# Two of three pairs of FFN input tiles as seven block products in place of eight, with the sums on VectorE and two accumulators to a PSUM bank

## The chip, the cores and the metric

The kernel runs on one core of one Trainium2 chip. The metric is the device time of one execution in microseconds (us). Three runs of the kernel before took 1320.02, 1320.15 and 1322.49 us; the median is 1320.15 us. The engines are TensorE (PE in the rows; PEld is its weight load), VectorE (DVE), ScalarE (ACT), GpSimd (POOL) and SyncE (SP), whose queue starts most transfers.

## The reference

One decoder layer on 512 tokens of width 1024 in float32: an FFN, a token mixer, a second FFN and an embedding stage, each with norms and a residual. The change is in the two FFNs:

```python
def rmsnorm(x, g):
    y = x * rsqrt(mean(x * x, axis=-1, keepdims=True) + EPS)
    return y * g

def swiglu(u, w_in, w_out):            # u 512x1024, w_in 1024x5632, w_out 2816x1024
    gate, up = split(u @ w_in, 2, axis=-1)
    return (silu(gate) * up) @ w_out

h = h + 0.5 * rmsnorm(swiglu(rmsnorm(h, ffn1_norm_pre), ffn1_w_in, ffn1_w_out), ffn1_norm_post)
h = h + rmsnorm(token_mixer(rmsnorm(h, mix_norm_pre), ...), mix_norm_post)
h = h + 0.5 * rmsnorm(swiglu(rmsnorm(h, ffn2_norm_pre), ffn2_w_in, ffn2_w_out), ffn2_norm_post)
```

## The kernel before, in words

**Three matmuls for one.** Every float32 operand is held as two parts, a rounded high part and the rest: `whi`/`wlo` of a weight chunk, `uhi`/`ulo` of the normed input. `wchunk` (L83) loads a chunk of 128x1024 over SP's queue into one of two `raw` buffers, ScalarE casts the high part (L91) and VectorE subtracts it for the low part (L92). `mm3` (L99) adds high by high, high by low and low by high into PSUM.

**The FFN.** `ffn` (L247) computes 22 pairs of tiles, f = 0 to 21: a gate tile and an up tile, each 128 hidden columns by 512 tokens. A tile takes one weight chunk: eight blocks of 128 input rows, three matmuls each, 24 matmuls of 512 columns into one bank (`pgu`, L282). `ev` (L252) follows: ScalarE applies Silu to the gate tile (L259), VectorE multiplies the up tile in (L262), ScalarE casts and VectorE subtracts the two parts of `hid` (L263, L266). The first tile pairs of an FFN (three in the first FFN, two in the second) go through `start_tiles` (L223) instead, token half by token half, in matmuls of 256 columns (tile `p` in the rows), because the input arrives by token blocks.

**The output projection.** `out_proj` (L168) multiplies `hid` by `wo`, two column halves of 11 chunks each; the first half takes the chunks as they come, with the parts in `vhi`/`vlo`, two buffers. Each chunk feeds 24 matmuls. The residual `h`, 512x1024, lies in SBUF (`h`, tag `hz`) through the FFN, and the two gain rows are loaded while f = 4 runs.

**What sets the order.** The program is written tile by tile, and a scheduler places the instructions of each engine into one list; each engine works through its list in order, and so does SP's queue. A buffer is written again when its last reader is done. PSUM has eight banks: four for tag `mm`, four for tag `ax`.

Of the kernel before, what the change touches and what calls it, by code (L numbers as in the profile page):

```python
# [32 lines left out]
def layer_kernel(ctx, tc, x, pT, wf1, wo1, wfm, wsm, wtm, wbr, wout, wf2, wo2, wgate, wproj,  # L33
# [198 lines left out]
    def sandwich_tail(h, ys, gn, u):  # L232
        def finish(tt, r):
            V.scalar_tensor_tensor(h[:, tt, :], ys[tt], r, h[:, tt, :], op0=ALU.mult, op1=ALU.add)
            make_u(tt, h, gn, u, ys[tt])
        return finish

# [9 lines left out]
    def ffn(fp, free, wf, wo, h, u, gi, gn_i, first):  # L247
        hid = [None] * FT
        marks = []
        g = {}  # L250

        def ev(f, part):  # L252
            def run(n, ps):
                if part == 0:
                    if f == 2 and len(first) == 6:
                        t = g[f] = lp.tile([128, T + 608], F32, name="gx")
                    else:
                        t = g[f] = sp.tile([128, T], F32, name="gt", tag="t512", bufs=2)
                    A.activation(t[:, n], ps[:, n], AF.Silu)  # L259
                else:  # L260
                    t = g[f]
                    V.tensor_tensor(t[:, n], ps[:, n], t[:, n], op=ALU.mult)  # L262
                    m = A.copy(hid[f][:, 0, n], t[:, n])  # L263
                    if f == 4:
                        marks.append(m)
# [9 lines left out]
        start_tiles([(w, 128, ev(i // 2, i % 2)) for i, w in enumerate(first)], u)  # L275
        for f in range(nf, FT):
            hid[f] = hid_tile(f)
            for i in range(2):
                w = wchunk(wf[2 * f + i])
# [12 lines left out]

        def load(ch, j, a):
            if a is None:
                dst = upper(fp)
# [7 lines left out]
        return u2  # L303

    hdram = dp.tile([128, 4, D], F32, name="hdram")
    gd = dp.tile([16, 128, T], F32, name="gd")
# [5 lines left out]
    with pool("s1", "right") as small:  # L312
        env.small = small
        f1_pool = ExitStack()
        fp = f1_pool.enter_context(pool("f1"))
        xt = [small.tile([128, D], F32, name=f"ys{i}") for i in range(2)]
        SY.dma_start(h[:, 0, :], x[0])
        SY.dma_start(cst[:, 0:C_TRI], consts[:, 0:C_TRI])
        SY.dma_start(h[:, 1, :], x[1])
        gn = small.tile([128, D], F32, name="gn")  # L320
        SY.dma_start(gn, gain_row(G_F1))
        weights = start_weights(fp, wf1, 6, 2)
        first = [next(weights)]
# [12 lines left out]
        u = ffn(fp, f1_pool.close, wf1, wo1, h, u, G_F1 + 1, G_MIX, first)  # L336
        for tt in range(4):
            SY.dma_start(hdram[:, tt, :], h[:, tt, :])

# [620 lines left out]
    if True:  # L960
        tl = tail_pool.enter_context(pool("tail"))
        mgh = tl.tile([128, KT, T], F32R, name="mgh")
        mgl = tl.tile([128, KT, T], F32R, name="mgl")
        gpt = small.tile([128, D], F32, name="gp")
        gnt = small.tile([128, D], F32, name="gn")
        ys = [small.tile([128, D], F32, name=f"ys{tt}") for tt in range(4)]
        h = hp.tile([128, 4, D], F32, name="h2", tag="hz")
        for tt in range(4):
            SY.dma_start(h[:, tt, :], hdram[:, tt, :])
        for m2 in range(4):  # L970
            wb = wchunk(wbr[4 + m2], dst=upper(tl))
# [149 lines left out]
```

## Time and profile before

| | us |
|---|---|
| median of three runs | 1320.15 |
| the profiled execution | 1320.2 |
| its span in the trace | 1318.4 |
| TensorE busy | 1287.5 |
| VectorE busy | 639.3 |
| ScalarE busy | 465.7 |

The span runs from the first instruction to the last; 1.8 us of the execution lie around it. The granted TensorE clock was 0.994 of full speed over the span. Matmuls are pipelined: a matmul's own duration holds the time in the pipe, and successive ones overlap. What a stream of them costs is read from the distance between their starts, or between events that stand once in each tile.

### The profile page before, as it was taken

To read this page: it belongs to the slowest core of one execution; us is meant where nothing else is said; L and a number is where in the kernel's file an instruction comes from. 1 tells how busy PE (TensorE), PEld (TensorE's weight loads), DVE (VectorE), ACT (ScalarE), POOL (GpSimd) and SP (SyncE) were. 2 spreads that over 40 slices of the span, in tenths; PEclk is the share of its full clock that TensorE was granted. 3 is DMA by queue.
4 is the path that set the end of the run, shared out by engine and by line. 5 is a ranking of instruction groups with operands and counts; after the bars stand their busy time and mean duration, and the time that the engine had idled before them with its cause. 6 is when DMAs were issued, how large, how long until landed. Compare 5 with 4: busy or idle time off the path is not lost.

```text
span 1318.4 us, 16647 instructions
## 1 busy us (share of the span) xinstructions
PE 1287.5 (98%) x6661; PEld 1074.3 (81%) x6661; DVE 639.3 (48%) x1088; ACT 465.7 (35%) x765; POOL 70.0 (5%) x71
## 2 busy tenths in 40 slices
PE   7999999999989999999999999989999999999997
PEld 6988888888879888877678888779888888888876
DVE  6233333323262699987686454463333333223465
ACT  6222222212253453454655222352222223112353
POOL 0000000000010000021002001220000000000000
PEclk9999999999999999999999999999999999999999
DMA  6243333223342223344206635522433333233431
GB/s 216 67 128 96 96 96 98 94 83 99 122 143 92 88 65 111 97 121 130 79 1 147 212 108 181 159 87 81 130 96 96 96 96 108 68 96 96 128 112 64
DMA packets 57772, 141.26 MB, mean 107 GB/s; under 512 B 17568, under 2 KB 20064, under 8 KB 57696
## 3 DMA queue, kind: packets, MB, share of 16 engines
q1 hardware_dynamic: 56688, 136.54, 33.9%
q10 hardware_dynamic: 1008, 3.67, 0.9%
q8 instruction: 52, 0.85, 0.3%
q14 instruction: 24, 0.20, 0.0%
HBM read 128.62 MB, written 11.57 MB: 106 GB/s over the span
## 4 chain that ended last, share of the span: by engine, by line
PE 86%; DMA 5%; DVE 5%; ACT 2%; issue 1%; POOL 0%; SPq 0%; DVEq 0%; POOLq 0%; ACTq 0%
PE pgu L101 11%; PE pgu L100 11%; PE pgu L102 11%; PE acc L101 5%; PE acc L102 5%; PE acc L100 5%; PE p L101 3%; PE p L100 3%; PE p L102 3%; PE ptm L101 2%; PE ptm L100 2%; PE ptm L102 2%; PE pg L100 2%; PE pg L102 2%; PE pg L101 2%; PE pat L713 2%
## 5 line engine op out<-in xcount | busy, mean ns | idle before, releaser
L91 ACT CAST whi<-raw 128x1024 fp32r<-128x1024 f32 x135 | 142.1, 1052 | 389.7 <-PE pgu L101 154.0
L92 DVE TENSOR_TENSOR wlo<-raw,whi 128x1024 fp32r<-128x1024 f32 x135 | 166.3, 1232 | 195.0 <-ACT whi L91 187.6
L100 PE MATMUL pgu<-uhi,whi 128*128 128x512 f32 x624 | 242.8, 389 | 0.0
L102 PE MATMUL pgu<-uhi,wlo 128*128 128x512 f32 x624 | 242.8, 389 | 0.0
L101 PE MATMUL pgu<-ulo,whi 128*128 128x512 f32 x624 | 242.7, 389 | 0.0
L100 PEld LDWEIGHTS pgu<-uhi,whi 128*128 128x128 f32 x624 | 117.1, 188 | 24.5
L102 PEld LDWEIGHTS pgu<-uhi,wlo 128*128 128x128 f32 x624 | 117.1, 188 | 24.4
L101 PEld LDWEIGHTS pgu<-ulo,whi 128*128 128x128 f32 x624 | 117.1, 188 | 24.0
L92 DVE TENSOR_TENSOR vlo<-raw,vhi 128x1024 fp32r<-128x1024 f32 x45 | 56.1, 1249 | 131.0 <-ACT vhi L91 130.9
L101 PE MATMUL acc<-vlo,hid 128*128 128x512 f32 x288 | 112.1, 389 | 0.0
L102 PE MATMUL acc<-vhi,hid 128*128 128x512 f32 x288 | 111.7, 389 | 0.0
L91 ACT CAST vhi<-raw 128x1024 fp32r<-128x1024 f32 x45 | 47.1, 1048 | 143.7 <-PE acc L102 123.3
L100 PE MATMUL acc<-vhi,hid 128*128 128x512 f32 x288 | 97.4, 389 | 0.0
L262 DVE TENSOR_TENSOR gt<-pgu,gt 128x512 f32<-128x512 f32 x39 | 27.0, 692 | 136.7 <-PE pgu L102 136.7
L78 POOL TENSOR_TENSOR rinv<-ms,mhalf 128x1 f32<-128x1 f32 x32 | 18.9, 594 | 844.0 <-DVE ms L123 844.0
L101 PEld LDWEIGHTS acc<-vlo,hid 128*128 128x128 f32 x288 | 54.1, 188 | 11.3
L100 PEld LDWEIGHTS acc<-vhi,hid 128*128 128x128 f32 x288 | 54.1, 188 | 11.2
L102 PEld LDWEIGHTS acc<-vhi,hid 128*128 128x128 f32 x288 | 54.0, 188 | 11.3
L101 PE MATMUL ptm<-wlo,uhi 128*128 128x512 f32 x128 | 50.3, 393 | 0.0
L100 PE MATMUL ptm<-whi,uhi 128*128 128x512 f32 x128 | 50.0, 395 | 0.0
L102 PE MATMUL ptm<-whi,ulo 128*128 128x512 f32 x128 | 49.8, 391 | 0.0
L100 PE MATMUL pg<-uhi,whi 128*128 128x512 f32 x104 | 41.2, 396 | 0.0
(394 smaller groups left out, 2335.9 us busy)
## 6 DMA issues: line engine op xcount, KB each, us to landing
raw<-wf SPq DMA_DIRECT2D x88, 512.0 KB, 3.6
raw<-wo SPq DMA_DIRECT2D x44, 512.0 KB, 3.6
raw<-wfm SPq DMA_DIRECT2D x28, 512.0 KB, 3.7
raw<-wtm SPq DMA_DIRECT2D x20, 512.0 KB, 3.7
gd<-gst SPq DMA_DIRECT2D x16, 256.0 KB, 2.1
raw<-wbr SPq DMA_DIRECT2D x8, 512.0 KB, 4.4
grl<-gd SPq DMA_DIRECT2D x16, 256.0 KB, 3.2
raw<-wout SPq DMA_DIRECT2D x8, 512.0 KB, 4.2
```

Source lines behind the costliest of these rows:

```text
L78: G.tensor_tensor(out_, in_, e, op=ALU.pow)
L91: A.copy(hi[:, :n], raw[:, :n])
L92: (eng or V).tensor_sub(lo[:, :n], raw[:, :n], hi[:, :n].bitcast(F32))
L100: PE.matmul(ps, l[0], r[0], start=start, stop=False)
L101: PE.matmul(ps, l[0], r[1], start=False, stop=False)
L102: PE.matmul(ps, l[1], r[0], start=False, stop=stop)
L262: V.tensor_tensor(t[:, n], ps[:, n], t[:, n], op=ALU.mult)
L713: PE.matmul(pa[:, :S], qbT[b:b + 64, pr, tt * 128:tt * 128 + 128], kbT[b:b + 64, pr, :S], start=True, stop=True)
```

## The change

Of f = 4 to 21, those with f % 3 = 0 stay as they were (6, 9, ... 21), and the other twelve of each FFN go through the new `Seven.pair`. There the gate chunk is cut into g1 (input rows 0 to 511) and g2 (512 to 1023), the up chunk into w1 and w2, and the input into b11, b21 (tokens 0 to 255) and b12, b22 (tokens 256 to 511). With

- S1 = w1 + w2, S2 = S1 - g1, S3 = g1 - w1, S4 = g2 - S2 (tiles `sa` and `sb`)
- T1 = b12 - b11, T2 = b22 - T1, T3 = T2 - b11, T4 = b21 - T2 (once per FFN, in `Seven.__init__`)

the seven products are g1 b11, g2 b21, S2 T2, S3 T3, S1 T1, w2 T4 and S4 b22, each of four blocks by three matmuls of 256 columns. They land in `pa` to `pd` (in the rows `pfa` to `pfd`), two to a bank but for the first, and VectorE adds them into `ct`. The parts are made by `parts`: ScalarE casts, VectorE subtracts. x1 are the parts of the gate chunk, x2 of `sa`, x3 of `sb`, x4 of w2.

Buffers: the parts take turns over three `whi`/`wlo` sets and one set in the output tiles' place (`xr`); raw chunks take turns over two `raw` and two `rawy`. T1 and T4 take the place of the residual (tag `hz`), which is read again after the last pair (`hr`, from `x` in the first FFN, from `hdram` in the second, where the mixer's tail now writes it). The gain rows are loaded there too, over SP's queue. The first two chunks of two output projections go to `whi`/`wlo`.

```diff
+    def parts(dst, src):
+        A.copy(dst[0], src)
+        V.tensor_sub(dst[1], src, dst[0].bitcast(F32))
+        return dst
...
+            V.tensor_tensor(t1, b12[0], b11[0], op=SUB)
+            V.tensor_tensor(t1, t1, b12[1], op=ADD)
+            V.tensor_tensor(t1, t1, b11[1], op=SUB)
+            V.tensor_tensor(t2, b22[0], t1, op=SUB)
+            V.tensor_tensor(t2, t2, b22[1], op=ADD)
+            parts(ts[1], t2)
...
+        def ring(self):
+            self.n[0] += 1
+            if self.n[0] % 4 == 0:
+                return [env.small.tile([128, 1024], F32R, name=f"xr{k}", tag=f"ys{2 + k}") for k in range(2)]
+            return [wp.tile([128, 1024], F32R, name=nm, tag=nm, bufs=3) for nm in ("whi", "wlo")]
...
+        def pair(self, f, wg, wu, hid):
+            g, w = self.load(wg), self.load(wu)
...
+            x1 = parts(self.ring(), g)
+            V.tensor_tensor(sa[:, H1], w[:, H1], w[:, H2], op=ALU.add)
+            V.tensor_tensor(sa[:, H2], sa[:, H1], g[:, H1], op=ALU.subtract)
+            x2 = parts(self.ring(), sa)
+            V.tensor_tensor(sb[:, H1], g[:, H1], w[:, H1], op=ALU.subtract)
+            V.tensor_tensor(sb[:, H2], g[:, H2], sa[:, H2], op=ALU.subtract)
+            x3 = parts(self.ring(), sb)
+            x4 = parts((x4[:, H1], x4[:, H2]), w[:, H2])
...
+            product(pa[:, N1], x1, 0, ub(0, N1))
+            A.copy(c[:, 0], pa[:, N1])
+            product(pb[:, N1], x1, 512, ub(4, N1))
+            product(pb[:, N2], x2, 512, tb(1))
+            V.tensor_tensor(c[:, 1:3], two(pb), bc(c[:, 0]), op=ALU.add)
+            product(pc[:, N1], x3, 0, tb(2))
+            product(pc[:, N2], x2, 0, tb(0))
+            V.tensor_tensor(c[:, 0::3], two(pc), bc(c[:, 2]), op=ALU.add)
+            V.tensor_tensor(c[:, 2], pc[:, N2], c[:, 0], op=ALU.add)
+            product(pd[:, N1], x4, 0, tb(3))
+            product(pd[:, N2], x3, 512, ub(4, N2))
+            V.tensor_tensor(c[:, 0::3], two(pd), c[:, 0::3], op=ALU.add)
+            t = sp.tile([128, 2, 256], F32, name="gt", tag="t512", bufs=2)
+            A.activation(t, c[:, 1::2], AF.Silu)
+            V.tensor_tensor(t, t, c[:, 0::2], op=ALU.mult)
...
+            parts((hid[f][:, 0], hid[f][:, 1]), t.rearrange("p a b -> p (a b)"))
...
         for f in range(nf, FT):
+            if f >= 4 and f % 3:
+                seven.pair(f, wf[2 * f], wf[2 * f + 1], hid)
+                continue
             hid[f] = hid_tile(f)
...
+            if f == 3:
+                seven = Seven(fp, u)
+
+        h = hp.tile([128, 4, D], F32, name="hr", tag="hz")
+        for tt in range(4):
+            SY.dma_start(h[:, tt, :], hsrc(tt))
         gp = env.small.tile([128, D], F32, name="gp")
         gn = env.small.tile([128, D], F32, name="gn")
-        with tc.issue_after(marks[0].ins):
-            A.dma_start(gp, gain_row(gi))
-            A.dma_start(gn, gain_row(gn_i))
+        SY.dma_start(gp, gain_row(gi))
+        SY.dma_start(gn, gain_row(gn_i))
```

VectorE's list in the first FFN, before, at the end of the start tiles (`gx` is the last of them) and at f = 3. `wlo` is the low part of a weight chunk (two for each f), `gt` the product of gate and up, `hid` its low part.

```order
L262 TENSOR_TENSOR gx<-p_547,gx 128x256
L266 TENSOR_TENSOR hid_244<-gx,hid_244 128x256
L92 TENSOR_TENSOR wlo<-raw,whi 128x1024
L262 TENSOR_TENSOR gt<-pgu,gt 128x512
L92 TENSOR_TENSOR wlo<-raw,whi 128x1024
L266 TENSOR_TENSOR hid_575<-gt,hid_575 128x512
```

From f = 3 on, four instructions stand there for each f. The same list now, at the pair f = 10 (its sums are `ct_1330`). L339, L342, L343 and L346 add up the banks of a pair; L253 are low parts, and `wlo<-sb` and `x_1436` are x3 and x4 of the next pair, f = 11.

```order
L339 TENSOR_TENSOR ct_1330<-pfb,ct_1330 128x512
L342 TENSOR_TENSOR ct_1330<-pfc,ct_1330 128x2x256
L343 TENSOR_TENSOR ct_1330<-pfc,ct_1330 128x256
L253 TENSOR_TENSOR wlo<-sb,whi 128x1024
L253 TENSOR_TENSOR x_1436<-rawy,x_1436 128x512
L346 TENSOR_TENSOR ct_1330<-pfd,ct_1330 128x2x256
L253 TENSOR_TENSOR wlo<-raw,whi 128x1024
L349 TENSOR_TENSOR gt<-gt,ct_1330 128x512
L308 TENSOR_TENSOR sa<-rawy 128x512
L311 TENSOR_TENSOR sb<-rawy 128x512
L253 TENSOR_TENSOR xr_1590<-raw,xr_1589 128x1024
```

The parts of the next pair now stand between the sums of the pair that runs, behind the sums of `pfc`; `wlo<-raw` and `xr` behind them are the two chunks of f = 12, and `sa` and `sb` those of f = 13.

SP's list through the first FFN, before (`cst` and `prm` are constants, `wf` the input chunks, `wo` those of the output projection, `wtm` the mixer's):

```order
L328 DMA cst<-consts 128x320
L329 DMA prm<-params 128x192
L85 DMA raw<-wf 128x1024 x42
L85 DMA raw<-wo 128x1024 x22
L85 DMA raw<-wtm 128x1024 x2
```

and now, where `rawy` are the chunks of f = 21, `gp` and `gn` the gain rows and `hr` the residual:

```order
L299 DMA rawy<-wf 128x1024 x2
L85 DMA raw<-wo 128x1024
L402 DMA gp<-gains 128x1024
L403 DMA gn<-gains 128x1024
L85 DMA raw<-wo 128x1024
L399 DMA hr<-x 128x1024 x4
L85 DMA raw<-wo 128x1024 x20
```

Six transfers stand between the last input chunk and the third chunk of the output projection, four of which wait for the last pair's products.

## Rows read from the trace of the kernel before

**Rows 1.** From the page: busy time of each engine with its share of the span, and the chain of work that ended last, by engine and by line.

```profile
PE 1287.5 (98%) x6661; PEld 1074.3 (81%) x6661; DVE 639.3 (48%) x1088; ACT 465.7 (35%) x765; POOL 70.0 (5%) x71
...
PE 86%; DMA 5%; DVE 5%; ACT 2%; issue 1%; POOL 0%; SPq 0%; DVEq 0%; POOLq 0%; ACTq 0%
PE pgu L101 11%; PE pgu L100 11%; PE pgu L102 11%; PE acc L101 5%; PE acc L102 5%; PE acc L100 5%; PE p L101 3%; PE p L100 3%; PE p L102 3%; PE ptm L101 2%; PE ptm L100 2%; PE ptm L102 2%; PE pg L100 2%; PE pg L102 2%; PE pg L101 2%; PE pat L713 2%
```

**Rows 2.** Two stretches of input tiles, one in each FFN. Columns: stretch and its length, busy us and instructions of PE, PEld, DVE, ACT and POOL, granted clock, DMA share, GB/s.

```profile
60.00:110.00 50.00, 50.00 (x222) 41.39 (x222) 17.89 (x20) 14.22 (x18) 0.00 (x0) 1.00 0.37 116
...
1000.00:1100.00 100.00, 100.00 (x443) 82.81 (x442) 35.64 (x39) 29.46 (x38) 0.00 (x0) 1.00 0.32 95
```

**Rows 3.** VectorE in order of time: the multiplication that follows the up tile, at f = 3 and at f = 18, 19 and 20 of the first FFN. Columns: start, duration, engine, line, operation, tiles, shapes, in brackets the idle time before and what ended it.

```profile
64.16 0.69 DVE L262 TENSOR_TENSOR gt<-pgu,gt 128x512 f32<-128x512 f32 x1 [3.42 <-PE pgu L102]
...
227.36 0.69 DVE L262 TENSOR_TENSOR gt<-pgu,gt 128x512 f32<-128x512 f32 x1 [3.38 <-PE pgu L102]
...
238.24 0.69 DVE L262 TENSOR_TENSOR gt<-pgu,gt 128x512 f32<-128x512 f32 x1 [3.38 <-PE pgu L102]
...
249.12 0.69 DVE L262 TENSOR_TENSOR gt<-pgu,gt 128x512 f32<-128x512 f32 x1 [1.72 <-PE pgu L102]
```

**Rows 4.** TensorE in order of time in the first FFN's start tiles, matmuls of 256 columns. From the first row to the last there are four chunks (`xh`, `xl`) of 24 matmuls, 96 starts; the last row is the next chunk's first.

```profile
24.21 0.28 PE L100 MATMUL p<-uhi,xh 128*128 128x256 f32 x1
24.33 0.28 PE L101 MATMUL p<-ulo,xh 128*128 128x256 f32 x1
24.45 0.28 PE L102 MATMUL p<-uhi,xl 128*128 128x256 f32 x1
...
35.60 0.28 PE L102 MATMUL p<-uhi,xl 128*128 128x256 f32 x1
35.72 0.28 PE L100 MATMUL p<-uhi,whi 128*128 128x256 f32 x1
```

**Rows 5.** The instructions of one tile over the whole span: durations in ns (shortest, median, longest), first and last start.

```profile
L100 PE MATMUL pgu<-uhi,whi x624: 389/389/398, 53.0 to 1129.3; 128*128 128x512 f32 x156
```

**Rows 6.** Groups of instructions by line and shape: busy us, mean ns of one, idle time before them and its releasers.

```profile
L92 DVE TENSOR_TENSOR wlo<-raw,whi 128x1024 fp32r<-128x1024 f32 x135 | 166.3, 1232 | 195.0 <-ACT whi L91 187.6 <-PE pg L102 1.8
L262 DVE TENSOR_TENSOR gt<-pgu,gt 128x512 f32<-128x512 f32 x39 | 27.0, 692 | 136.7 <-PE pgu L102 136.7
L266 DVE TENSOR_TENSOR hid<-gt,hid 128x512 fp32r<-128x512 f32 x39 | 26.7, 685 | 1.4 <-ACT hid L263 1.4
L262 DVE TENSOR_TENSOR gt<-p,gt 128x256 f32<-128x256 f32 x8 | 3.4, 422 | 9.0 <-PE p L102 9.0
L91 ACT CAST whi<-raw 128x1024 fp32r<-128x1024 f32 x135 | 142.1, 1052 | 389.7 <-PE pgu L101 154.0 <-issue 124.8 <-PE pc L101 35.6
L263 ACT CAST hid<-gt 128x512 fp32r<-128x512 f32 x39 | 24.2, 621 | 11.2 <-DVE gt L262 11.2
L259 ACT ACTIVATE gt<-pgu 128x512 f32<-128x512 f32 x39 | 22.9, 588 | 6.4 <-PE pgu L102 6.4
L259 ACT ACTIVATE gt<-p 128x256 f32<-128x256 f32 x8 | 3.0, 379 | 4.9 <-PE p L102 4.9
```

**Rows 7.** DMA issues: tiles, queue, number, size of one, median us to landing.

```profile
raw<-wf SPq DMA_DIRECT2D x88, 512.0 KB, 3.6
...
h<-x SPq DMA_DIRECT2D x4, 512.0 KB, 6.3
gp<-gains ACTq DMA_DIRECT2D x4, 512.0 KB, 4.2
...
h<-hdram SPq DMA_DIRECT2D x4, 512.0 KB, 6.9
```

**Rows 8.** The stretch of the first FFN from the last block of its input to the end of f = 3, columns as in rows 2.

```profile
26.50:64.10 37.60, 37.60 (x272) 35.69 (x271) 10.95 (x18) 9.83 (x18) 0.00 (x0) 1.00 0.28 84
```

**Rows 9.** VectorE in the second FFN: the last block of its input, and the multiplication of f = 3.

```profile
898.72 1.29 DVE L166 TENSOR_TENSOR ulo<-put,uhi 128x512 fp32r<-128x512 f32 x2 [2.19 <-ACT uhi L165]
...
934.41 0.69 DVE L262 TENSOR_TENSOR gt<-pgu,gt 128x512 f32<-128x512 f32 x1 [3.42 <-PE pgu L102]
```

**Rows 10.** ScalarE in the first output projection: casts of successive chunks, each released by a chunk's matmuls.

```profile
276.30 1.05 ACT L91 CAST vhi<-raw 128x1024 fp32r<-128x1024 f32 x1 [4.35 <-PE acc L102]
281.74 1.05 ACT L91 CAST vhi<-raw 128x1024 fp32r<-128x1024 f32 x1 [4.39 <-PE acc L102]
```

**Rows 11.** TensorE's waits at the start of the mixer's output projection.

```profile
836.16 0.73 PE L100 MATMUL acc<-vhi,mgh 128*128 128x512 f32 x2 [1.21 <-ACT vhi L91]
837.42 0.50 PE L101 MATMUL acc<-vlo,mgh 128*128 128x512 f32 x1 [0.52 <-DVE vlo L92]
```

More of the change, by code (lines that the diff above doesn't have):

```diff
@@ L230, in start_tiles, with sandwich_tail @@
                 ev(n, ps)
-    def sandwich_tail(h, ys, gn, u):
+    def sandwich_tail(h, ys, gn, u, spill=False):
         def finish(tt, r):
             V.scalar_tensor_tensor(h[:, tt, :], ys[tt], r, h[:, tt, :], op0=ALU.mult, op1=ALU.add)
+            if spill:
+                SY.dma_start(hdram[:, tt, :], h[:, tt, :])
             make_u(tt, h, gn, u, ys[tt])
@@ L245, in start_weights, with __init__, at, load @@
             yield wchunk(wf[i], dst=dst, eng=G if wf is wf2 and i > 1 else None)
-    def ffn(fp, free, wf, wo, h, u, gi, gn_i, first):
+    H1, H2 = slice(0, 512), slice(512, 1024)
+    def parts(dst, src):
+        A.copy(dst[0], src)
+        V.tensor_sub(dst[1], src, dst[0].bitcast(F32))
+        return dst
+    class Seven:
+        def __init__(self, fp, u):
+            self.fp, self.u = fp, u
+            SUB, ADD = ALU.subtract, ALU.add
+            def at(k, n):
+                return u[0][:, k:k + 4, n].bitcast(F32), u[1][:, k:k + 4, n].bitcast(F32)
+            b11, b21, b12, b22 = at(0, SEG[0]), at(4, SEG[0]), at(0, SEG[1]), at(4, SEG[1])
+            raw = [env.small.tile([128, 4, 256], F32, name=f"tr{t}", tag=t) for t in ("gp", "gn", "ys0", "ys1")]
+            t1, t2, t3, t4 = raw
+            hz = hp.tile([128, 4, 4, 256], F32R, name="t14", tag="hz")
+            ts = [(hz[:, 0], hz[:, 1])] + [tuple(t.rearrange("p (k n) -> p k n", n=256) for t in upper(fp))
+                                           for _ in range(2)] + [(hz[:, 2], hz[:, 3])]
+            V.tensor_tensor(t1, b12[0], b11[0], op=SUB)
[4 more added lines that the diff above has]
+            parts(ts[1], t2)
+            V.tensor_tensor(t3, t2, b11[0], op=SUB)
+            V.tensor_tensor(t3, t3, b11[1], op=SUB)
+            parts(ts[2], t3)
+            parts(ts[0], t1)
+            V.tensor_tensor(t4, b21[0], t2, op=SUB)
+            V.tensor_tensor(t4, t4, b21[1], op=ADD)
+            parts(ts[3], t4)
+            self.t = ts
+            self.n = [0, 0]
+        def ring(self):
[3 more added lines that the diff above has]
+            return [wp.tile([128, 1024], F32R, name=nm, tag=nm, bufs=3) for nm in ("whi", "wlo")]
+        def load(self, src):
+            self.n[1] += 1
+            t = (wp.tile([128, 1024], F32, name="raw", tag="raw", bufs=2) if self.n[1] % 4 in (1, 2) else
+                 env.small.tile([128, 1024], F32, name="rawy", tag=f"ys{(self.n[1] + 1) % 4}"))
+            SY.dma_start(t, src)
+            return t
+        def pair(self, f, wg, wu, hid):
+            g, w = self.load(wg), self.load(wu)
+            sa = env.small.tile([128, 1024], F32, name="sa", tag="gp")
+            sb = env.small.tile([128, 1024], F32, name="sb", tag="gn")
+            x4 = lp.tile([128, 1024], F32R, name="x4", tag="gx")
+            x1 = parts(self.ring(), g)
[6 more added lines that the diff above has]
+            x4 = parts((x4[:, H1], x4[:, H2]), w[:, H2])
+            N1, N2 = SEG
+            def product(ps, x, c, b):
+                for k in range(4):
+                    mm3(ps, cols(x, c + k * 128, c + k * 128 + 128), b(k), k == 0, k == 3)
+            def tb(i):
+                return lambda k: (self.t[i][0][:, k], self.t[i][1][:, k])
+            def ub(k0, n):
+                return lambda k: u_at(self.u, k0 + k, n)
+            def two(ps):
+                return ps.rearrange("p (a b) -> p a b", b=256)
+            def bc(a):
+                return a[:, None, :].to_broadcast([128, 2, 256])
+            c = self.fp.tile([128, 4, 256], F32, name=f"ct{f}", tag=f"hid{f}")
+            pa, pb, pc, pd = mmp("pfa"), axp("pfb"), mmp("pfc"), axp("pfd")
+            product(pa[:, N1], x1, 0, ub(0, N1))
[13 more added lines that the diff above has]
+            V.tensor_tensor(t, t, c[:, 0::2], op=ALU.mult)
+            hid[f] = self.fp.tile([128, 2, T], F32R, name=f"hid{f}")
+            parts((hid[f][:, 0], hid[f][:, 1]), t.rearrange("p a b -> p (a b)"))
@@ L248, in ffn @@
+    def ffn(fp, free, wf, wo, hsrc, u, gi, gn_i, first):
         hid = [None] * FT
-        marks = []
         g = {}
@@ L262, in run @@
                     V.tensor_tensor(t[:, n], ps[:, n], t[:, n], op=ALU.mult)
-                    m = A.copy(hid[f][:, 0, n], t[:, n])
-                    if f == 4:
-                        marks.append(m)
+                    A.copy(hid[f][:, 0, n], t[:, n])
                     V.tensor_sub(hid[f][:, 1, n], t[:, n], hid[f][:, 0, n].bitcast(F32))
@@ L275, in ffn @@
         start_tiles([(w, 128, ev(i // 2, i % 2)) for i, w in enumerate(first)], u)
+        seven = None
         for f in range(nf, FT):
+            if f >= 4 and f % 3:
+                seven.pair(f, wf[2 * f], wf[2 * f + 1], hid)
+                continue
             hid[f] = hid_tile(f)
             for i in range(2):
-                w = wchunk(wf[2 * f + i])
+                if seven is None:
+                    w = wchunk(wf[2 * f + i])
+                else:
+                    w = parts(seven.ring(), seven.load(wf[2 * f + i]))
                 ps = mmp("pgu")
@@ L293, in load @@
         def load(ch, j, a):
+            dst = None
             if a is None:
-                dst = upper(fp)
+                if ch or j > 1:
+                    dst = upper(fp)
             else:
@@ L302, in ffn @@
                  ys, gp, sandwich_tail(h, ys, gn, u2), free)
-        return u2
+        return h, u2
     hdram = dp.tile([128, 4, D], F32, name="hdram")
@@ L335, in layer_kernel @@
                 make_u(tt, h, gn, u, xt[tt % 2])
-        u = ffn(fp, f1_pool.close, wf1, wo1, h, u, G_F1 + 1, G_MIX, first)
+        h, u = ffn(fp, f1_pool.close, wf1, wo1, lambda tt: x[tt], u, G_F1 + 1, G_MIX, first)
         for tt in range(4):
@@ L997, in layer_kernel @@
     fp = f2_pool.enter_context(pool("f2"))
-    u = ffn(fp, f2_pool.close, wf2, wo2, h, u, G_F2 + 1, G_PLE, list(start_weights(fp, wf2, 4, 2)))
+    h, u = ffn(fp, f2_pool.close, wf2, wo2, lambda tt: hdram[:, tt, :], u, G_F2 + 1, G_PLE, list(start_weights(fp, wf2, 4, 2)))
     pt_ = [t.rearrange("p (k t) -> p k t", t=T) for t in wchunk(pT)]
```

4 lines of the change are left out of this document (2 added, 2 removed).

## The prediction

> **What bounds the kernel now.** I read the busy shares first, then the chain of waits, then stretches of the stages that the change touches, then single rows there. TensorE is busy 98% of the span and holds 86% of the chain, a third of the span with the tiles `pgu` alone [rows 1]. VectorE is busy 48%. In the input tiles TensorE has no gap at all at granted clock 1.00, while VectorE works 17.9 us of 50 and ScalarE 14.2 [rows 2]. So these stages end by TensorE's own stream: a change there gains what it takes out of that stream, as long as the other engines keep ahead of it. VectorE today sits waiting for the up tile's last matmul, 3.4 us a time [rows 3]; that room is what the change spends.
>
> Durations are from the profiled execution: 1320.2 us, of which 1318.4 are span and 1.8 lie around it. It stands within 0.1 us of the median, so the sum applies to either.
>
> **The stream.** A pair of tiles as it is: the multiplication at f = 20 comes 184.96 us after that at f = 3, 17 pairs, so 10.880 us for 48 matmuls of 512 columns, 0.2267 us each [rows 3]. In 256 columns: 96 matmuls from 24.21 to 35.72, 0.1199 us each [rows 4]. A row's own 0.28 or 0.39 us holds the pipe and is not the price [rows 4, 5]. Taken together, 256 columns more cost 0.1068 us, which is 2.4 GHz, and some 0.013 us come on top of every matmul, whatever its width. Seven products are 84 matmuls of 256 columns: 10.07 us. So a pair saves 0.81 us (7.4%, not the 12.5% of seven for eight, since 36 more matmuls pay the 0.013). Twelve pairs in each of two FFNs: 24 x 0.809 = 19.4 us. The start matmuls load a new 128-column weight each as the products will, so the weight loads are in the 0.1199 already.
>
> The Trainium skill's page "TensorE: Matmul & The Clock Gate", section "Back-to-back issue gap", gives N/2.4 + 2.5 ns at the full clock, 215.8 and 109.2 ns for these widths. By it a pair would save 48 x 0.2158 - 84 x 0.1092 = 1.19 us (an estimate from the page), 28.5 us in all. The trace does not agree: it has 226.7 and 119.9.
>
> **VectorE's and ScalarE's new work.** One new pair on VectorE: three low parts of 1024 at 1.232; four sums of 512 in SBUF, x4's low part, the product and `hid`'s low part, seven at 0.685; three additions of 512 out of PSUM at 0.692 and one of 256 at 0.422 [rows 6]. That is 3.70 + 4.80 + 2.08 + 0.42 = 11.00 us, against 3.84 for a pair as it was (2 x 1.232 + 0.692 + 0.685). It is more than TensorE's 10.07, but every third f stays: over three f VectorE has 2 x 11.00 + 3.84 = 25.8 us, TensorE 2 x 10.07 + 10.88 = 31.0. No row has an addition with a repeated operand or a stepped output; I take 0.692, the same shape out of PSUM, and bound it from 0.4 (the 256 row) to 1.23 (a pass of 1024): eight per cycle, so 23.5 to 30.1 us of 31.0. ScalarE has per pair three casts at 1.052, two at 0.621, Silu 0.588 and a copy of 256 at 0.379: 5.4 us [rows 6]. It is no bound.
>
> Whether it is in time is read from the order. Count from the start of the first of two pairs; its products end at 1.4, 2.9, 4.3, 5.8, 7.2, 8.6 and 10.1. The additions of `pfc` wait until 7.2 and take 1.1, then x3 of the next pair is done at 9.6, x4 at 10.2, the addition of `pfd` at 10.9. The next pair asks for x3 at its fourth product, 10.1 + 4.3 = 14.4: 4.8 us to spare, the least that I find in the cycle (x1, x2, x4 and the chunks of the whole tile have 5 or more). Behind that stand `sa` and `sb` of f + 3. Their up chunk goes into the buffer that x4's low part freed at 10.2, so with 3.6 us to landing [rows 7] it is there at 13.9; VectorE comes to it at 13.1 and waits about 1 us, with x3 and x4 already behind it. The rest runs to 30, and the multiplication of the whole tile waits for 31.0: VectorE closes the cycle with about 1 us to spare, TensorE never waits. The four turns of parts and four banks per tag come free at least a product ahead of their next use. Cost: 0; with that cover gone, the x3 of a pair costs its cast and low part, 2.28 us.
>
> **The start.** T1 to T4 need the whole input: eight passes and four low parts of 1024, 14.8 us. In the first FFN that falls into the stretch 26.5 to 64.1 us, where VectorE has 10.95 us of work in 37.6 [rows 8], 26.7 free. With x1, x2, x4 and the sums of the first pair (5.9) and the second's x1 and half its sums (2.6) I get 23.3 us: 3.4 to spare. x3 comes last: its buffer is freed by the end of f = 3 at 63.9 (the first `pgu` at 53.0 plus 10.88 [rows 5]), so cast, multiplication, low part: 66.2, and the fourth product asks for it at 63.9 + 4.3 = 68.2. Cost: 0, bounded by 0 and 5 us. In the second FFN the input is complete at 900.0 and f = 3 ends at 934.4 [rows 9], as long a stretch with fewer start tiles: 0 to 3.
>
> **The output projections.** `hr` waits on SP's queue for the last pair; six transfers stand there instead of none. At f = 21 TensorE has 10.88 us of work, then two chunks of 5.44 [rows 10] whose loads are issued before or among them. So the third chunk is wanted 21.8 us after the last pair, cast and low part less, 19.5. Four residual transfers took 6.3 and 6.9 us to landing with neighbours, gain rows 4.2 [rows 7]; six one behind the other at 3.6, not even overlapped, would be 21.6, and they do overlap. I take 0, bound 0 to 4 in each FFN. The gain rows are wanted only after 11 chunks, 60 us on. In the mixer's tail the first two chunks get buffers earlier; TensorE waited there 1.21 + 0.52 us [rows 11]: a gain of up to 1.7, but `grl` transfers now stand behind two more chunk loads on SP's queue, so -1.7 to +2; I take 0. The writes of `hdram` and later reads stand where nothing waits for them within 40 us.
>
> **Sum.** 1320.2 - 19.4 = 1300.8 us.
>
> **Rivals.**
> *VectorE lags now and then.* The same cycle with its 1 us of spare used up and x3 late at times, or late first pairs and third chunks as bounded above: VectorE's cycle at 31.7 in place of 31.0, over 12 cycles, is 8.4 us: 1309. For it: VectorE at 83% in order with three waits per pair. Against it: 4.8 us of cover at the narrowest place.
> *No fixed part.* If the 0.013 us are hidden behind something that the products lack, a pair costs seven eighths of 10.88: 1.36 us less, 32.6 in all: 1287.6. Rows 4 speak against it. The Trainium skill's rule named above would give 1291.7 for the same reason.
> *The products cost more.* At 0.1295 us a matmul (10.88/84) nothing is left: 1320. Every product starts with new operands and two waits on other engines; but the start tiles do too, every 24 matmuls.
> *VectorE becomes the bound: slower.* Its waits in a new pair are not overlapped: 2.2 us from `pfb` to `pfc`, 0.6 for Silu between sum and product, twice, and 3.4 for the whole tile [rows 3, 6]. 25.8 + 9.0 = 34.8 us for three f, where 32.6 were: 12 x 2.2 = 26 us more, 1346. It decides from 6.8 us of waits in a cycle on, or additions of 1.54 us each. Against it: the order puts other work into those waits.
>
> **How the numbers follow.** Forecast 0.70, VectorE lagging 0.13, no fixed part 0.04, products dearer 0.05, VectorE the bound 0.08. The forecast's own range is 1296 to 1305: 4 us down for the mixer's 1.7 and 1% of the new stream (2.4), 4 up for half the bounds of the starts. To hold 8 in 10 it reaches up over most of the second case: 1296 to 1313. A measurement of this kernel tells 0.2% (2.6 us) from no change. Faster: 0.70 + 0.13 + 0.04 = 0.87; same 0.05; slower 0.08.
>
> **What would show it.** Twelve pairs per FFN at 10.07 us, multiplications (`gt<-gt,ct`) 31.0 us apart over three f; TensorE without idle time in the input tiles, the first product of f = 4 at 63.9; VectorE at 80 to 85% there, its longest wait that for the whole tile's end; additions of 512 near 0.69. Wrong would be: TensorE's waits for `wlo` or `whi` at a fourth product (VectorE too slow), a gap at f = 4 (the sums T), a gap at the third chunk of the projection (SP's queue), or products of more than 1.45 us without waits (the matmuls' price).

## The result and the profile after

| | before | after |
|---|---|---|
| median of the runs, us | 1320.09 | 1298.67 |
| range, us | 1318.91 to 1322.49 | 1295.99 to 1301.68 |
| profiled execution, us | 1320.2 | 1301.68 |
| its span, us | 1318.4 | 1299.9 |

The ratio is 0.9836 [0.981, 0.9863]: 21.4 us less, where 19.4 were forecast. The profiled execution of after is the longest of its four, which matters below: its span is only 18.5 us shorter. Four executions (one each of before, e1, e6 and e7, of e7 the profiled one) ran at a mean granted clock of 0.96 to 0.97, and the ratios leave them out.

The page's busy times after, to be set beside [rows 1]:

```profile
PE 1266.7 (97%) x7525; PEld 1096.9 (84%) x7525; DVE 825.0 (63%) x1354; ACT 523.5 (40%) x845; POOL 71.1 (5%) x71
```

TensorE has 864 matmuls more and 20.8 us less to do (24 pairs of 84 for 48: exactly 864). VectorE took on 185.7 us, 7.7 for each pair with the T sums shared out, and TensorE nevertheless sets the end of these stages.

Two stretches of input tiles, one in each FFN, columns as in [rows 2]:

```profile
60.00:240.00 180.00, 180.00 (x1280) 169.08 (x1279) 139.36 (x186) 79.00 (x105) 0.00 (x0) 1.00 0.33 106
930.00:1100.00 170.00, 170.00 (x1223) 160.28 (x1222) 132.52 (x179) 75.53 (x100) 0.00 (x0) 1.00 0.33 106
```

The first busy figure equals the stretch: still no gap on TensorE, at granted clock 1.00 (2.4 GHz). VectorE is at 77 and 78%.

VectorE in order of time, the multiplication of the whole tile, which comes every three f and answers to [rows 3]:

```profile
64.02 0.69 DVE L367 TENSOR_TENSOR gt<-pgu,gt 128x512 f32<-128x512 f32 x1 [1.98 <-PE pgu L102]
...
94.63 0.69 DVE L367 TENSOR_TENSOR gt<-pgu,gt 128x512 f32<-128x512 f32 x1 [1.61 <-PE pgu L102]
...
125.40 0.69 DVE L367 TENSOR_TENSOR gt<-pgu,gt 128x512 f32<-128x512 f32 x1 [2.16 <-PE pgu L102]
...
217.48 0.69 DVE L367 TENSOR_TENSOR gt<-pgu,gt 128x512 f32<-128x512 f32 x1 [2.16 <-PE pgu L102]
```

From 64.02 to 217.48 there are five cycles of three f: 30.69 us each, where before took 3 x 10.88 = 32.64 and 31.0 were forecast. In brackets VectorE waits for TensorE's last matmul, 1.6 to 2.2 us: it arrives before TensorE in every cycle of both FFNs but the last, where the multiplication at f = 21 follows other work and TensorE does not wait for it either.

TensorE in order of time: a pair's first product, the next pair's, and the whole tile behind them, whose place answers to [rows 4, 5]:

```profile
94.44 0.28 PE L100 MATMUL pfa<-uhi,whi 128*128 128x256 f32 x1
...
95.87 0.28 PE L100 MATMUL pfb<-uhi,whi 128*128 128x256 f32 x1
...
104.37 0.28 PE L100 MATMUL pfa<-uhi,xr 128*128 128x256 f32 x1
...
105.73 0.28 PE L100 MATMUL pfb<-uhi,xr 128*128 128x256 f32 x1
...
114.17 0.40 PE L100 MATMUL pgu<-uhi,whi 128*128 128x512 f32 x1
...
125.13 0.28 PE L100 MATMUL pfa<-uhi,whi 128*128 128x256 f32 x1
```

A pair starts at 94.44, the next at 104.37, the whole tile at 114.17 and the next cycle at 125.13: 9.93, 9.80 and 10.96 us. A product is twelve matmuls. With weights in `whi` twelve starts take 1.43 us (94.44 to 95.87, 0.119 each); with weights in `xr` they take 1.36 (104.37 to 105.73, 0.113). Columns and data types are the same in both.

TensorE's five longest waits over the whole span after (total us, times, longest):

```profile
PE put L108 <- DVE ys L132: 7.3, 1, 7.3
PE put L108 <- DVE ys L156: 5.6, 3, 3.3
PE pc L100 <- ACT DT L766: 3.6, 1, 3.6
PE acc L100 <- DVE grl L1098: 2.7, 1, 2.7
PE p L101 <- DVE ulo L166: 2.3, 1, 2.3
```

From the first pair on, no wait is in the input tiles or the output projection of either FFN. The `put` and `pc` waits lie outside the changed code, in the norms and the mixer. The one for `grl` is at the start of the mixer's output projection, where the waits of [rows 11] stood; the last one is in the second FFN's start tiles and is taken up under e6.

**Where the time went.** I subtract start times of the same instruction in the two traces. First the one after, by tile (shortest, median and longest duration, first and last start):

```profile
L100 PE MATMUL acc<-whi,hid x32: 394/394/399, 247.9 to 1122.8; 128*128 128x512 f32 x32
L100 PE MATMUL ptm<-whi,uhi x128: 387/389/478, 423.4 to 698.3; 128*128 128x512 f32 x128
L102 PE MATMUL pgu<-uhi,xr x96: 388/388/398, 89.4 to 1112.1; 128*128 128x512 f32 x96
```

And before:

```profile
L100 PE MATMUL acc<-vhi,hid x288: 387/389/390, 259.7 to 1227.3; 128*128 128x512 f32 x144
L100 PE MATMUL ptm<-whi,uhi x128: 387/389/478, 434.0 to 706.5; 128*128 128x512 f32 x128
L102 PE MATMUL pgu<-uhi,wlo x624: 389/389/398, 53.5 to 1129.8; 128*128 128x512 f32 x156
```

And TensorE's first matmul of f = 4 in the second FFN, before and after:

```profile
934.14 0.39 PE L100 MATMUL pgu<-uhi,whi 128*128 128x512 f32 x1
```

```profile
928.13 0.28 PE L100 MATMUL pfa<-uhi,whi 128*128 128x256 f32 x1
```

From the first matmul of f = 4 to the first of the output projection TensorE takes 195.85 us before (63.89 to 259.74 and 934.14 to 1129.99) and 184.16 after (63.75 to 247.91 and 928.13 to 1112.29), in both FFNs alike. So the input tiles gave 11.7 us in each FFN, 23.4 in all. Between the FFNs this execution lost some of it again: the first projection starts 11.8 us earlier, the mixer's first `ptm` 10.6, f = 4 of the second FFN only 6.0. That loss of 5.8 us was not in the forecast; it is taken up under e6 and at the end. (Behind the second FFN 0.8 us came back, which makes up the 18.5.)

### The profile page after: what moved, and what is told of

Its sections match the earlier page's. It is cut to its first block, busy times and chain, and to the rows that moved or that the text cites. A ratio compares the mean times of both kernels' runs of the same rounds, so it can differ in the third digit from the quotient of the medians.

```text
span 1299.9 us, 18739 instructions
## 1 busy us (share of the span) xinstructions
PE 1266.7 (97%) x7525; PEld 1096.9 (84%) x7525; DVE 825.0 (63%) x1354; ACT 523.5 (40%) x845; POOL 71.1 (5%) x71
## 5 line engine op out<-in xcount | busy, mean ns | idle before, releaser
L91 ACT CAST whi<-raw 128x1024 fp32r<-128x1024 f32 x69 | 72.5, 1051 | 131.0 <-PE pc L101 36.4
L92 DVE TENSOR_TENSOR wlo<-raw,whi 128x1024 fp32r<-128x1024 f32 x69 | 85.5, 1238 | 61.4 <-ACT whi L91 53.0
L102 PE MATMUL acc<-vhi,hid 128*128 128x512 f32 x256 | 99.6, 389 | 0.0
L100 PE MATMUL acc<-vhi,hid 128*128 128x512 f32 x256 | 86.9, 389 | 0.0
L100 PE MATMUL pgu<-uhi,whi 128*128 128x512 f32 x144 | 56.2, 390 | 0.0
L101 PE MATMUL pgu<-ulo,whi 128*128 128x512 f32 x144 | 56.2, 390 | 0.0
L102 PE MATMUL pgu<-uhi,wlo 128*128 128x512 f32 x144 | 56.0, 389 | 0.0
L252 ACT CAST whi<-sb 128x1024 fp32r<-128x1024 f32 x24 | 25.2, 1049 | 52.7 <-PE pfc L101 38.6
L100 PE MATMUL pc<-uhi,whi 128*128 128x512 f32 x96 | 38.7, 404 | 3.6 <-ACT DT L766 3.6
L102 PE MATMUL pg<-uhi,wlo 128*128 128x512 f32 x104 | 40.9, 393 | 0.0
L101 PE MATMUL pg<-ulo,whi 128*128 128x512 f32 x104 | 40.7, 392 | 0.0
```

The costliest lines, as they stand in the source:

```text
L91: A.copy(hi[:, :n], raw[:, :n])
L92: (eng or V).tensor_sub(lo[:, :n], raw[:, :n], hi[:, :n].bitcast(F32))
L100: PE.matmul(ps, l[0], r[0], start=start, stop=False)
L101: PE.matmul(ps, l[0], r[1], start=False, stop=False)
L102: PE.matmul(ps, l[1], r[0], start=False, stop=stop)
L252: A.copy(dst[0], src)
```

## Experiments

Three questions were open. Is the gain the missing eighth product, or would narrow matmuls and new buffers alone have given it? How much room has VectorE really? And what sets the price of a matmul of 256 columns? e1 to e4 ran beside before at 1320.51 us, e5 to e8 beside before at 1321.57.

**e1: eight products in place of seven.** The pairs keep their 256-column matmuls, their buffers and their place, but compute gate and up as eight plain block products; the sums and the T are gone.

```diff
-            x1 = parts(self.ring(), g)
...
+            xs = (parts(self.ring(), g), parts(self.ring(), w))
...
+                for n in SEG:
+                    for k in range(KT):
+                        mm3(ps[:, n], cols(x, k * 128, (k + 1) * 128), u_at(self.u, k, n), k == 0, k == KT - 1)
```

> The same twelve f of each FFN, their chunks loaded and cast as in the changed kernel, but eight plain block products in matmuls of 256 columns, with no sums, no T tiles and no seven. If the gain is that twelve matmuls out of 96 are gone, a pair takes 96 x 0.118 to 0.120 = 11.3 to 11.5 us, 0.4 to 0.6 more than the 10.88 of whole tiles, and the time is 1320 + 24 x 0.5 = 1330 to 1335 us. If the gain came from the deeper buffers or from narrower matmuls, it stays at or below 1320.

Measured: ratio 1.013 [1.0104, 1.0156]; three executions of 1331.44 to 1339.65 us, 11 to 19 slower than before, the highest a little above what was expected. The traces are sharper than these times. From the first matmul of f = 4 to the first of the output projection TensorE takes 201.89 us in e1, 195.85 before and 184.16 after, in both FFNs alike. Halving the width of the matmuls thus costs 6.0 us an FFN, 12.1 in all, and the missing product gives 17.7, 35.5 in all: 1.48 for each of the 24 pairs, where twelve matmuls at 0.118 are 1.42. So the gain is the product left out, and it first has to pay for the finer split. Narrow matmuls and new buffers alone made the kernel slower.

**e2: all three tiles of a cycle in pairs.** By the prediction's sums VectorE would need 11.0 us in a pair against TensorE's 10.07, so this kernel should be bound by VectorE.

```diff
-            if f >= 4 and f % 3:
+            if 4 <= f < 21:
```

> Seven products for every f from 4 to 20, not two of three; all sums on VectorE. If VectorE's durations add up (11.00 us a pair against TensorE's 9.9), VectorE becomes the bound: 17 x 11.0 + 10.9 = 198 us of input tiles where there are 184, +28 us in both FFNs: about 1327. If what counts is VectorE's distance from start to start (0.60 us for 512 and 1.14 for 1024 in the trace after, 9.8 us a pair), TensorE stays the bound but for in-order waits: 1289 (five more pairs in each FFN at 0.97 us) to 1300.

Measured: 1292.69 us, ratio 0.9791 [0.9776, 0.9807]; faster than after. A stretch of its input tiles, columns as in [rows 2]:

```profile
75.00:225.00 150.00, 149.74 (x1267) 149.54 (x1266) 142.06 (x203) 74.55 (x104) 0.00 (x0) 1.00 0.31 103
```

VectorE is busy 95% and TensorE has still only 0.26 us of gaps in 150. How that goes together with 11.0 us in a pair of 9.9, VectorE's rows in order of time show:

```profile
107.71 0.69 DVE L312 TENSOR_TENSOR sb<-rawy,sa 128x512 f32<-128x512 f32 x1
108.31 0.69 DVE L346 TENSOR_TENSOR ct<-pfd,ct 128x512 f32<-128x512 f32 x1
108.92 1.22 DVE L253 TENSOR_TENSOR wlo<-sa,whi 128x1024 fp32r<-128x1024 f32 x1
110.05 0.69 DVE L339 TENSOR_TENSOR ct<-pfb,ct 128x512 f32<-128x512 f32 x1
```

An instruction of 0.69 us is followed 0.60 us later by the next, one of 1.22 us after 1.13. The durations overlap at their ends, so a column of them overstates what the engine needs. From start to start a pair needs 3 x 1.13 + 10 x 0.60 + 0.34 (the 256-wide addition) = 9.7 us, against the 9.93 that TensorE takes for a pair of e2 on average. The hint stood in [rows 9]: "x2" with 1.29 us for two passes that take 0.685 each, so 0.60 apart.

The ten further pairs gave 6.0 us in the medians, where 10.96 - 9.93 for each would be 10. The traces have 180.24 us from the first pair to the output projection, against 184.16 after: 3.9 an FFN, 7.8 in all. Part of the rest is that the pairs themselves became dearer, 9.93 us each where after's average 9.87. The remaining 2 us between 7.8 and 6.0 are within the spread of after (5.7 us).

**e3: e2 with the four weight sums on GpSimd.** If VectorE's room decides, taking 2.4 us a pair off it should help.

```diff
-            V.tensor_tensor(sa[:, H1], w[:, H1], w[:, H2], op=ALU.add)
+            G.tensor_tensor(sa[:, H1], w[:, H1], w[:, H2], op=ALU.add)
...
-            V.tensor_tensor(sb[:, H2], g[:, H2], sa[:, H2], op=ALU.subtract)
+            G.tensor_tensor(sb[:, H2], g[:, H2], sa[:, H2], op=ALU.subtract)
```

> As e2_all, with the four weight sums of a pair on GpSimd (four at about 1.62 us, 6.5 us a pair). If VectorE alone held e2_all back, TensorE is the bound: 10 more pairs at 0.97 us, 1289. If GpSimd's sums slow VectorE's down, or its longer chain from chunk to sum comes late, it lies above 1298 and the rows show VectorE's passes over 0.69 or TensorE's waits for x2 and x3.

Measured: 1293.28 us, ratio 0.9798 [0.9783, 0.9814], the same as e2, and neither of the two times expected. TensorE had hardly a gap left to close. But VectorE got no room either: it does 136 passes fewer and is busy 879.1 us against 880.6. Its groups in e3 (busy us, mean ns, idle before):

```profile
L349 DVE TENSOR_TENSOR gt<-gt,ct 128x512 f32<-128x512 f32 x34 | 56.3, 1657 | 0.0
L346 DVE TENSOR_TENSOR ct<-pfd,ct 128x512 f32<-128x512 f32 x34 | 23.1, 680 | 1.1 <-PE pfd L102 1.1
```

The same groups in e2:

```profile
L349 DVE TENSOR_TENSOR gt<-gt,ct 128x512 f32<-128x512 f32 x34 | 23.4, 689 | 1.5 <-ACT gt L348 1.4
L346 DVE TENSOR_TENSOR ct<-pfd,ct 128x512 f32<-128x512 f32 x34 | 23.4, 688 | 0.0
```

The product of gate and up, with both inputs in SBUF, went from 0.689 to 1.657 us (`hid`'s low part, of the same kind, from 0.688 to 1.324); the addition with one input in PSUM stayed at 0.68. The Trainium skill's page "SBUF — State Buffer", section "Who interferes with whom", says that a VectorE instruction with two SBUF inputs contends with a GpSimd instruction that reads SBUF. These rows agree, and give a price: up to 2.4 times in the mean of a group.

**e4 and e5: what sets the matmul's price.** In after, `xr` holds the weights of every second pair. e4 lets the first of the two pairs have it; e5 puts the pool of `whi` and `wlo` at the other end of SBUF.

```diff
-            if self.n[0] % 4 == 0:
+            if self.n[0] % 4 == 1:
```

```diff
-    wp = ctx.enter_context(tc.tile_pool(name="wp", bufs=3))
+    wp = ctx.enter_context(tc.tile_pool(name="wp", bufs=3, side="right"))
```

> Only the turn of the part buffers is moved: the set in the output tiles' place (xr) serves x1 of the first pair of two, not of the second. In the trace after, matmuls of 256 columns start 0.113 us apart with weights in xr and 0.120 with weights in whi, both with the input as moving operand. If the place of the weights sets that, the first pair's pfa goes to 0.113 and the second's to 0.120, and f % 3 = 0 loses its xr half (0.230 to 0.227). If the position in the cycle sets it (what the other engines do then), the second pair keeps 0.113. The time stays within 2 us of 1298.7 either way.

> The changed kernel with the pool of the raw chunks and of whi and wlo at the other end of SBUF, nothing else. Matmuls of 256 columns start 0.120 us apart with weights in whi and the input as moving operand, 0.117 with T2 and T3 as moving operand, 0.113 with weights in xr, which lies at the other end. If the distance in SBUF between weights and moving operand sets that price, whi with the input falls to about 0.113 and the time by up to 24 x 84 x 0.005 = 10 us, 1289; if not, the 0.120 stays and the time is 1299.

Measured: e4 1299.13 us, ratio 0.9841 [0.9825, 0.9857]; e5 1303.74, ratio 0.987 [0.985, 0.989]. A product of the first pair in e4, with weights in `xr`, and the start of the next:

```profile
94.50 0.28 PE L100 MATMUL pfa<-uhi,xr 128*128 128x256 f32 x1
...
95.91 0.28 PE L100 MATMUL pfb<-uhi,xr 128*128 128x256 f32 x1
```

That is 0.118 for each of twelve; the same product of the second pair, with weights in `whi`, takes 0.120 (104.42 to 105.86). So the 0.113 stayed neither with `xr` nor with the second pair: neither expectation held. Over all products of e4 those with `xr` start every 0.118 to 0.120 us, those with `whi` every 0.117 to 0.120. In e5 u with `whi` takes 0.118 in all pairs but the first of an FFN (0.113), u with `xr` 0.118, and a whole tile 11.00 us where it was 10.96. It is not the execution that makes the difference: e6, whose input tiles are those of after, has after's prices again, 0.113 for u with `xr` (as have e1, e2, e3 and e8):

```profile
104.27 0.28 PE L100 MATMUL pfa<-uhi,xr 128*128 128x256 f32 x1
...
105.63 0.28 PE L100 MATMUL pfb<-uhi,xr 128*128 128x256 f32 x1
```

That the price changes when only places and turns of buffers change is measured; the rule behind it stays open. It is small: from the first pair to the output projection TensorE takes 184.97 us in e4 and 185.10 in e5, against 184.16, so under 2 us for both FFNs. The other 3 us by which e5's median lies above after's are not explained by the input tiles; the two ratios' intervals overlap.

**e6: the mixer's first chunks as before.** The change lets the mixer's output projection, like those of the FFNs, load its first two weight chunks into other buffers. This run takes that edit alone back.

```diff
-        out_proj(4, lambda ch, j, a: wchunk(wout[ch, j], dst=xo.get(a) or (upper(tl) if ch or j > 1 else None)),
+        out_proj(4, lambda ch, j, a: wchunk(wout[ch, j], dst=xo.get(a) or upper(tl)),
```

> The changed kernel with one part undone: the mixer's output projection takes its first two chunks into vhi and vlo again, as before. In the trace after, TensorE waits there 2.7 us for the sum in grl, in that before 1.2 + 0.5 for vhi and vlo. If the chunk loads that stand ahead of grl on SP's queue made the new wait, it goes back to the old two and the time falls by about 1 us, less than a comparison of times can tell (1298); if the wait is set elsewhere, 2.7 stays.

Measured: 1297.09 us, ratio 0.9818 [0.9797, 0.9839]: not told apart from after by time. The waits tell it. TensorE at the start of that projection, in order of time; e6:

```profile
825.61 0.73 PE L100 MATMUL acc<-vhi,mgh 128*128 128x512 f32 x2 [1.12 <-ACT vhi L91]
826.87 0.50 PE L101 MATMUL acc<-vlo,mgh 128*128 128x512 f32 x1 [0.53 <-DVE vlo L92]
```

and after:

```profile
826.70 0.48 PE L100 MATMUL acc<-whi,mgh 128*128 128x512 f32 x1 [2.75 <-DVE grl L1098]
```

With the edit taken back the two waits of [rows 11] return (1.65 us) and the one for `grl` (2.75) is gone, as expected: the edit took out two waits and made one that is 1.1 us longer than both. On SP's queue two chunk loads stand ahead of the `grl` transfers in after (816.33 and 820.23), one in e6 (813.65 and 815.63).

The edit cost more further on. At the start of the second FFN, after, VectorE and GpSimd:

```profile
876.55 6.39 POOL L92 TENSOR_TENSOR xl<-raw,xh 128x1024 fp32r<-128x1024 f32 x2
877.31 3.39 DVE L234 SCALAR_TENSOR_TENSOR h<-ys,rinv,h 128x1024 f32<-128x1024 f32 x1
```

and the same VectorE pass in e6, where GpSimd's two were done at 879.4:

```profile
879.96 1.28 DVE L234 SCALAR_TENSOR_TENSOR h<-ys,rinv,h 128x1024 f32<-128x1024 f32 x1 [1.87 <-POOL rinv L78]
```

The pass reads two inputs from SBUF and runs beside a GpSimd pass that reads SBUF, as in e3: 3.39 us in place of 1.28. The low part `ulo` stands behind it, and TensorE waits 2.3 us for that. The pass takes 3.38 to 3.40 us in after, e1 to e5, e7 and e8, which all have the edit, and 1.28 in before and e6, which have not. From the last matmul ahead of the mixer's output projection (`pya`) to f = 4 of the second FFN it is 102.4 us before, 104.6 after and 102.3 in e6. So the edit cost 2.3 us: 1.1 at the projection and 1.2 behind it.

**e7: e2 with one pass more on VectorE.** x1's low part is made twice, the same values; this measures the room directly.

```diff
             x1 = parts(self.ring(), g)
+            V.tensor_sub(x1[1], g, x1[0].bitcast(F32))
```

> e2_all with x1's low part made twice, one more pass of 1024 on VectorE (1.14 us from start to start) in each of 34 pairs. In e2_all VectorE is busy 166 of 176 us and TensorE waits 0.26. If VectorE is at its limit there, TensorE now waits for it: need 9.3 to 9.8 plus 1.14, 10.4 to 10.9 us a pair against TensorE's 9.86, 34 x 0.6 to 1.0 = 20 to 35 us more than e2_all, 1312 to 1328. If there is still room, 1293 to 1296.

Measured: 1315.55 us, ratio 0.9957 [0.9941, 0.9973]; 22.9 us more than e2 (22 by the two ratios), or 0.67 for each of its 34 pairs. A stretch of its first FFN, columns as in [rows 2]:

```profile
104.00:184.00 80.00, 76.95 (x640) 75.94 (x638) 78.74 (x111) 36.86 (x53) 0.00 (x0) 1.00 0.32 102
```

VectorE is busy 98% and TensorE has 3 us of gaps, at granted clock 1.00. From start to start such a pass costs 1.13 us, so on average 1.13 - 0.67 = 0.46 us of it found room. In a pair of e2 the starts leave 9.93 - 9.7 = 0.2; the first four pairs of e7 still take 9.8 to 10.0 us, so a lead that VectorE has at the start probably pays for the rest. The rival in which VectorE is the bound is real: it lies less than one pass beyond e2.

**e8: e2 with the last tile paired too, and the residual's loads later.** The output projection's residual is loaded behind its seventh chunk instead of ahead of all of them, since the last pair holds the buffer longer.

```diff
-            if f >= 4 and f % 3:
+            if f >= 4:
...
-        for tt in range(4):
-            SY.dma_start(h[:, tt, :], hsrc(tt))
...
+            if not ch and j == 6:
+                for tt in range(4):
+                    SY.dma_start(h[:, tt, :], hsrc(tt))
```

> e2_all with f = 21 too as seven products and the residual's four transfers issued with the seventh chunk of the output projection in the program. One more pair in each FFN at 10.88 - 9.9 = 0.98 us: 1290.7 if nothing waits. Rival: the third and fourth chunk of the output projection come late, since the last pair no longer has a whole tile behind it under which the transfers run: TensorE waits for vhi at its start, up to 5 us in each FFN, 1293 to 1301.

Measured: 1291.21 us, ratio 0.9775 [0.9757, 0.9793]: 30 us less than before and near the 1290.7 expected. It is the lowest median, but its interval overlaps that of e2. From its first pair into the output projection TensorE has 0.26 us of gaps in 186:

```profile
64.00:250.00 186.00, 185.74 (x1540) 184.00 (x1539) 174.18 (x246) 90.92 (x125) 0.00 (x0) 1.00 0.34 112
```

## Why the prediction was right

The likeliest case came, 2.1 us below its 1300.8, inside its own range. The mechanism held; the sizes of some steps were off, and that the total came so close is in part luck.

- **The stream as the bound: right.** No gap in the input tiles, and e1 shows that the gain is the product left out: 1.48 us a pair.
- **The price of a product: right in kind, too high.** The 0.1199 us was read from start tiles [rows 4]. The products ran at 0.113 to 0.120, and a cycle's two pairs averaged (9.93 + 9.80)/168 = 0.1174. That is 0.2 us less for a pair than 10.07, 4.8 us in all. The whole tiles took 10.96 in place of 10.88, 1.0 us over twelve. Together 19.4 + 4.8 - 1.0 = 23.2, against 23.4 from the start times.
- **The rival without a fixed part: fell.** 256 columns at 2.4 GHz are 0.107 us; no product came below 0.113. By the formula of the Trainium skill's page "TensorE: Matmul & The Clock Gate", section "Back-to-back issue gap", it would be 0.109, and these rows don't bear that out either. The page calls it the gap of an isolated matmul and says itself that at small widths it is too low for a stream with weight loads, which the prediction left out.
- **VectorE's cycle: right in outcome, wrong in size.** I added durations, 11.0 us a pair and 25.8 of 31.0 in a cycle, and found about 1 us to spare. It was 9.7 a pair, since instructions start before the one ahead has ended; VectorE is busy 77 and 78% where 80 to 85 were forecast, and the waits for the whole tile show 1.6 to 2.2 spare. The error was on the safe side here. It would have ruled out e2 and e8, the better kernels. (The bounds for the additions also took all eight of a cycle at 0.692, though two are 256 wide; with these at 0.422 they are 24.0 to 30.7 of 31.0, and nothing changes.)
- **The single additions: right.** Repeated operand and stepped output cost nothing: 0.684 us for `pfb`, 0.691 for `pfc`, 0.692 for `pfd`, where I took 0.692 out of 0.4 to 1.23. VectorE's rows by line (shortest, median, longest):

```profile
L339 DVE TENSOR_TENSOR ct<-pfb,ct x24: 681/684/687, 68.9 to 1096.6; 128x512 f32<-128x512 f32 x24
L342 DVE TENSOR_TENSOR ct<-pfc,ct x24: 683/691/693, 71.3 to 1098.7; 128x512 f32<-128x512 f32 x24
L346 DVE TENSOR_TENSOR ct<-pfd,ct x24: 684/692/693, 74.1 to 1101.5; 128x512 f32<-128x512 f32 x24
```

- **The start at no cost: right.** x3's low part ended at 66.03 (66.2 was worked out); its product starts at 68.03, and TensorE never waits:

```profile
64.80 1.23 DVE L253 TENSOR_TENSOR wlo<-sb,whi 128x1024 fp32r<-128x1024 f32 x1
```

- **The up chunk's late landing: right, and hidden.** VectorE waits for it behind x3 and x4, as worked out (about 1 us):

```profile
108.28 0.69 DVE L308 TENSOR_TENSOR sa<-raw 128x512 f32<-128x512 f32 x1 [0.88 <-DMA raw<-wf]
```

- **The FFNs' output projections at no cost: right but for 0.3 us each.** There is no wait. But the first two chunks, now in `whi`, take 0.233 us a matmul where they took 0.227 in `vhi`.
- **The mixer's tail taken as 0: too low.** The wait at the projection grew by 1.0 us (2.75 for 1.73), inside the bounds of -1.7 to +2 and by the mechanism named, `grl` behind two more chunk loads. The 1.2 us that the same edit cost at the start of the second FFN (e6) were not foreseen, and with them it is 2.2, just outside.

The total came closer than its terms: 4.0 us more gain in the input tiles than forecast stand against losses between the FFNs, 5.8 us in the profiled execution. This is the luck in it. The three other executions were 2 to 6 us shorter; where, no trace shows.

## What to carry to other kernels

Read an engine's need from start to start, in a stretch where it runs without waits, and not as a sum of durations: 0.69 us of duration was 0.60 of VectorE's time, and that decides whether a third of the work can move there. Cutting a product out of a TensorE-bound stage pays as the stream shortens, once the finer split has been paid for: in the input tiles e1 priced the split at 12 us here, and the product left out gave 35. Moving small sums to GpSimd is no relief for VectorE while its own passes read two inputs from SBUF. And a side edit is best taken back alone and followed in the trace past its own place: half of what the mixer's edit cost came 50 us behind it.

## What the runs showed of the hardware

**The price of a matmul changes with the places and turns of its operands' buffers.** Same columns, same type: 0.113 to 0.120 us for 256 columns as the mean of a product, and 0.227 to 0.233 for 512. It came back unchanged in another execution with the same buffers (e6). In the input tiles e4 and e5 changed the time by under 2 us. The cause is open.

**VectorE's passes with two SBUF inputs grow beside GpSimd.** In e3 0.689 us became 1.657, in after 1.28 became 3.39.

**The granted clock fell in after where before kept it, though TensorE's work ahead of it was nearly the same.** Between the first FFN and the mixer TensorE waits in pieces for the norm. Stretches of 4 us, columns as in [rows 2]; after:

```profile
368.00:372.00 4.00, 2.97 (x18) 2.29 (x17) 3.82 (x7) 0.98 (x3) 0.87 (x2) 1.00 0.09 38
372.00:376.00 4.00, 2.78 (x14) 1.84 (x13) 2.66 (x5) 3.87 (x7) 0.55 (x1) 1.00 0.32 131
376.00:380.00 4.00, 2.89 (x13) 2.27 (x11) 4.00 (x7) 3.54 (x7) 0.00 (x0) 0.69 0.46 120
380.00:384.00 4.00, 4.00 (x17) 3.23 (x16) 2.94 (x5) 1.76 (x3) 1.06 (x1) 0.88 0.60 179
```

and before, the same place some 12 us later:

```profile
380.00:384.00 4.00, 2.70 (x16) 2.05 (x16) 3.87 (x7) 0.91 (x2) 0.81 (x2) 1.00 0.09 36
384.00:388.00 4.00, 2.81 (x14) 1.85 (x13) 2.65 (x5) 3.94 (x7) 0.55 (x1) 1.00 0.32 131
388.00:392.00 4.00, 2.89 (x16) 2.28 (x15) 4.00 (x7) 3.53 (x7) 0.00 (x0) 1.00 0.56 144
```

TensorE's busy 2.97, 2.78 and 2.89 us stand against 2.70, 2.81 and 2.89. In after the clock then went to 0.69 and 0.88, means between 2.4 and 1.2 GHz, and the two stretches lost (0.31 + 0.12) x 4 = 1.7 us of full clock. Over 34 us around this place the mean granted clock is 1.00 in the profiled executions of before, e1, e4 and e5, and 0.95 in those of after, e2, e3, e6 and e8, nothing in between; the operations there are the same in all of them. What decides it stays open. With one trace of each kernel it is not shown either that the kernel decides it, and not the single execution.

The 5.8 us lost between the FFNs are accounted for by place. From the first output projection to the mixer's first `ptm` it is 1.3 us, where the clock dips. From there to the mixer's `pat` it is 2.4: the wait for `pc` is 3.6 us in place of 2.5, and the granted clock over the 60 us around it is 0.94 in place of 0.97. From `pya` to the second FFN it is 2.2, the edit that e6 takes back. The first two lie in stages that the change leaves alone: a difference of a few us between two such kernels can come from there.
